# A hybrid decoder block on one core: a quarter of the expert rows streamed and multiplied densely in place of gathered

## The chip, the cores and the metric

The kernel runs on one core of one Trainium2 chip. The metric is device time in microseconds, the median of several executions. PE is the matmul engine, PEld its weight loads, DVE the vector engine, ACT the scalar engine, POOL the engine that issues gathers, SP the engine that issues most plain DMAs.

## The reference

For 256 tokens of width 2048 the layer computes, in float32:

```
h = rms_norm(x, norm1_g);  z = h @ w_in
x = x + (sigmoid(gA) * pool_mixer(z) + sigmoid(gB) * sgu_mixer(z)) @ w_out
h = rms_norm(x, norm2_g)
idx, gate = product_key_top16(h @ w_q, sub_keys)       # 8 heads x 16 experts per token
act = gelu(h . expert_u[idx])                          # 128 picks per token
x = x + sum_e gate_e * act_e * expert_v[idx_e]
out = rms_norm(x, final_g)
```

There are 128 x 128 = 16384 experts; expert number = 128 * first key + second key. A row of `expert_u` or `expert_v` is 2048 float32 numbers, 8 KB.

## The kernel before

Weights come from HBM in float32 tiles of 128 x 1024 through the class `Stream` (L54 to L109): SP loads a raw tile, ACT copies each half into a rounded part `hi` (L94), DVE or POOL subtracts it to get the rest `lo` (L96), and a product is made of three single-pass matmuls (`mm3` L243, `mm3a` L248), or of two, a wide one over both activation parts and a narrow one (`mm2` L253). Four raw buffers and five buffers of each part keep the stream ahead of PE; parts are made four halves ahead.

The stages follow one another: w_v, the pool mixer (the loop that calls `run_b` at L410, whose two partial sums `joined` L275 adds on ACT and DVE, while a layer norm runs beside it on DVE), the gate stages, w_out, and w_q (the queries). In the w_q stage `token_rows` (L731) transposes the last 48 tokens back to rows and copies each group of 16 to eight partition groups by seven DMAs from the ACT queue (L748), and `scores` (L754) hands the scores of each head to `topk_head` (L565), in two halves of 128 tokens: tokens 128 to 255 first, tokens 0 to 127 kept in the list `second`. `finish_topk` (L595) turns the picks into gather indices.

Then the sweep: all of `expert_u` streams through PE for the 208 first tokens (`run_u` L783, 128 keys of 128 experts) and the scores go to `s_scratch` in HBM (`evac` L801). The last 48 tokens do without the dense scores: their rows of `expert_u` are gathered and multiplied on DVE (L672), and their rows of `expert_v` are gathered and multiplied on PE.

After the sweep, the tail. One job per token (`v_job` L680): POOL issues a gather of 128 rows of `expert_v`, 1 MB (`fetch` L643), PE multiplies them with the coefficients in eight matmuls (L688). Beside it POOL fetches, for a token further on, its 128 scores out of `s_scratch` with a gather of 4-byte elements (`element` L837); 16 tokens make a group, whose coefficients DVE and ACT compute (`coefs` L649) and whose result is normed and written (`square` L700). First come what is left of the last 48 tokens, then tokens 128 to 207, then 0 to 127. The loop at L871 sets the order: `step` (L187) issues the PE work of the oldest fetched job and the gathers of the next, four gathers ahead, in five row buffers; `work` (L203) then takes pieces of work from the list `side` against a credit in estimated microseconds. The second top-k is put into `side` when the tail begins.

## Time and profile before

| | us |
|---|---|
| median of 3 runs | 1946.9 (1944.74 to 1947.67) |
| the profiled execution | 1951.77 |
| its span in the profile | 1950.0 |
| PE busy | 1662.7 (85%) |
| PEld busy | 1217.8 (62%) |
| DVE busy | 1033.1 (53%) |
| ACT busy | 717.4 (37%) |
| POOL busy | 595.9 (31%) |

The span is what the profiler saw between the first and the last instruction; the 1.8 us around it are part of the execution's time. A busy share is an average over stages that differ, so the rows further down are cut by stage: the mixers and queries up to some 602 us, the sweep from there to 1300 us, the tail from 1300 us to the end. The granted clock (PEclk) is 1.0 at 2.4 GHz and 0.5 at 1.2 GHz; a value between is a mean over both.

### The profile page before, as it was taken

What the parts mean: (1) busy time and instruction counts of PE and PEld (TensorE: products, weight loads), DVE (VectorE), ACT (ScalarE), POOL (GpSimd) and SP (SyncE); (2) the same over time, 40 slices, a digit from 0 to 9 for tenths busy, and PEclk for the clock granted to TensorE, in tenths of its full rate; (3) what the DMA queues carried; (4) which work ended last, traced back from release to release, by engine and by line L of the source; (5) the groups of instructions that cost most, each with busy time, mean ns of one, the idle gap of its engine ahead of it and who ended that gap; (6) DMA issues with size and microseconds to landing.
All of it is one profiled execution on the core that took longest, in us unless ns stands there. A gap on an engine that the chain in (4) does not pass through costs nothing.

```text
span 1950.0 us, 28018 instructions
## 1 busy us (share of the span) xinstructions
PE 1662.7 (85%) x10242; PEld 1217.8 (62%) x10242; DVE 1033.1 (53%) x2115; ACT 717.4 (37%) x1408; POOL 595.9 (31%) x609
## 2 busy tenths in 40 slices
PE   9999999999998999999999999985666666566665
PEld 7778888888998898888998899951110111011111
DVE  7887777777788787667676666763600000000000
ACT  7546555555434444544455445430010000000000
POOL 0220000000546111111111111136666656666662
PEclk9999999999999999999999999996576666667666
DMA  8556555555576999899999999988999999999998
GB/s 285 169 158 192 188 188 189 190 187 183 186 176 198 362 348 347 333 340 341 351 341 344 345 346 341 363 307 299 364 354 357 369 356 367 358 368 362 377 366 334
DMA packets 137994, 581.73 MB, mean 298 GB/s; under 512 B 21488, under 2 KB 37872, under 8 KB 98480
## 3 DMA queue, kind: packets, MB, share of 16 engines
q0 software_dynamic: 50704, 320.22, 42.8%
q1 hardware_dynamic: 86480, 256.97, 38.1%
q10 hardware_dynamic: 672, 2.75, 1.0%
q8 instruction: 80, 1.31, 0.3%
q14 instruction: 58, 0.48, 0.1%
HBM read 561.39 MB, written 15.73 MB: 296 GB/s over the span
## 4 chain that ended last, share of the span: by engine, by line
PE 33%; issue 30%; DMA 18%; DVE 8%; POOL 8%; ACT 1%; ACTq 0%; another core or an unknown queue 0%; SPq 0%; DVEq 0%; POOLq 0%
PE acc L792 13%; DMA rows<-in_exp_v,idxV 9%; DMA raw<-in_exp_u 8%; PE acc L793 6%; PE y L688 5%; POOL se L843 4%; POOL rows L645 4%; DVE lo L96 3%; PE acc L244 1%; PE acc L246 1%; PE acc L245 1%; PE acc L796 1%; ACT hi L94 1%; PE acc L250 1%; DVE rows L672 1%
## 5 line engine op out<-in xcount | busy, mean ns | idle before, releaser
L96 DVE TENSOR_TENSOR lo<-raw,hi 128x512 fp32r<-128x512 f32 x852 | 574.4, 704 | 288.0 <-ACT hi L94 273.8
L94 ACT CAST hi<-raw 128x512 fp32r<-128x512 f32 x904 | 535.3, 621 | 425.4 <-DMA raw<-in_exp_u 157.0
L792 PE MATMUL acc<-hhl,hi 128*128 128x416 f32 x1920 | 598.9, 372 | 3.8 <-ACT hi L94 3.8
L688 PE MATMUL y<-rows,cd 128*32 128x512 f32 x2048 | 400.1, 867 | 206.7 <-DMA rows<-in_exp_v,idxV 178.7
L793 PE MATMUL acc<-hhl,lo 128*128 128x208 f32 x1920 | 500.4, 261 | 17.8 <-DVE lo L96 17.3
L645 POOL DMA_INDIRECT rows<-in_exp_v,idxV x256 | 248.7, 972 | 513.2 <-DVE rows L672 310.7
L793 PEld LDWEIGHTS acc<-hhl,lo 128*128 128x128 f32 x1920 | 369.9, 193 | 27.5 <-DVE lo L96 26.7
L792 PEld LDWEIGHTS acc<-hhl,hi 128*128 128x128 f32 x1920 | 364.7, 190 | 35.7 <-ACT hi L94 29.1
L688 PEld LDWEIGHTS y<-rows,cd 128*32 128x32 f32 x2048 | 57.2, 130 | 502.9 <-DMA rows<-in_exp_v,idxV 376.2
L258 PE MATMUL acc<-hhl,hi 128*128 128x512 f32 x768 | 271.0, 397 | 1.9 <-ACT hi L94 1.8
L843 POOL DMA_INDIRECT se<-s_scratch,idxS x208 | 197.8, 951 | 65.5 <-issue 61.6
L260 PE MATMUL acc<-hhl,lo 128*128 128x256 f32 x720 | 202.5, 281 | 5.4 <-DVE lo L96 5.4
L654 DVE TENSOR_TENSOR cx<-se,rstd 128x16 f32<-128x16 f32 x13 | 2.3, 179 | 367.0 <-DMA se<-s_scratch,idxS 295.4
L258 PEld LDWEIGHTS acc<-hhl,hi 128*128 128x128 f32 x768 | 142.7, 188 | 32.3 <-ACT hi L94 2.9
L655 ACT ACTIVATE cx<-cx 128x16 f32<-128x16 f32 x16 | 3.5, 217 | 411.0 <-DVE cx L654 357.1
L260 PEld LDWEIGHTS acc<-hhl,lo 128*128 128x128 f32 x720 | 135.9, 189 | 10.0 <-DVE lo L96 8.4
L645 POOL DMA_INDIRECT rows<-in_exp_rows,idxU x48 | 52.4, 1092 | 228.9 <-DVE rows L672 122.5
L538 POOL DMA_DIRECT2D keys<-in_keysT x1 | 0.6, 563 | 370.1 <-PE acc L304 370.1
L672 DVE SCALAR_TENSOR_TENSOR rows<-rows,h2n 128x2048 f32<-128x2048 f32 x48 | 109.6, 2284 | 0.0
L714 DVE RECIPROCAL rt<-rt 128x1 f32<-128x1 f32 x16 | 2.6, 164 | 174.4 <-ACT rt L713 151.6
L96 POOL TENSOR_TENSOR lo<-raw,hi 128x512 fp32r<-128x512 f32 x52 | 71.9, 1394 | 64.9 <-ACT hi L94 57.0
L258 PE MATMUL acc<-mhl,hi 128*128 128x512 f32 x256 | 89.0, 395 | 0.0
(191 smaller groups left out, 1752.4 us busy)
## 6 DMA issues: line engine op xcount, KB each, us to landing
raw<-in_exp_u SPq DMA_DIRECT2D x256, 512.0 KB
raw<-in_w_in SPq DMA_DIRECT2D x96, 512.0 KB
raw<-in_w_out SPq DMA_DIRECT2D x32, 512.0 KB
raw<-in_w_q SPq DMA_DIRECT2D x32, 512.0 KB
s_scratch<-es SPq DMA_DIRECT2D x32, 416.0 KB
raw<-in_w_gproj SPq DMA_DIRECT2D x16, 512.0 KB
raw<-in_w_v SPq DMA_DIRECT2D x15, 512.0 KB
rows<-in_exp_v,idxV POOLq DMA_INDIRECT x256
```

Source lines behind the costliest of these rows:

```text
L94: self.nc.scalar.copy(h, t)
L96: eng.tensor_sub(l, t, h.bitcast(F32))
L244: nc.tensor.matmul(ps, whi, ahi, start=first, stop=False)
L245: nc.tensor.matmul(ps, whi, alo, start=False, stop=False)
L258: nc.tensor.matmul(ps, whi, both, start=first, stop=last)
L260: nc.tensor.matmul(ps[:, :T], wlo, act[:, 0], start=False, stop=False)
L645: nc.gpsimd.indirect_dma_start(out=r, out_offset=None, in_=src, in_offset=bass.IndirectOffsetOnAxis(ap=idx, axis=0))
L672: V.scalar_tensor_tensor(r, r, 1.0, h2n[g], op0=ALU.mult, op1=ALU.mult, accum_out=act[g][:, n:n + 1])
L688: nc.tensor.matmul(y[q * GQ:(q + 1) * GQ], cd[:, m * GQ:(m + 1) * GQ], r[:, q * 512:(q + 1) * 512], start=(m == 0), stop=(m == GT - 1))
L792: nc.tensor.matmul(o2, whi[:, w], hhl[:, k, :, 0:ND], start=(k == 0), stop=False)
L793: nc.tensor.matmul(o1, wlo[:, w], hhl[:, k, 0, 0:ND], start=False, stop=False)
L843: nc.gpsimd.indirect_dma_start(out=se[t0][:, m:m + 1], out_offset=None, in_=flat, in_offset=bass.IndirectOffsetOnAxis(ap=idxS[:, t0 + m:t0 ...
```

## The change

Rows of `expert_v` of the last 32 first keys (experts 12288 to 16383, 33.6 MB) are no longer gathered for the first 208 tokens. The gathers of those tokens have a bounds check that skips such rows, and a coefficient `gM` that is zero for them. In their place the 32 x 128 rows stream through a second `Stream`, and `dense_part` multiplies them for all 208 tokens at once: it builds one-hot tables on DVE (`at`, `bt`) and turns them into a dense gate table on PE (52 pieces of four tokens), reads the stored scores of these keys back from HBM (8 chunks, 3.4 MB), and makes 128 pieces of six matmuls each. The tail's loop issues 1.6 credits of these pieces at every step. Groups of tokens that end before the dense part is done are copied out of PSUM to SBUF (at most nine) and finished later, one every three steps (`release`), with an addition of the dense result by matmul (`add_dense`). Of the eight PSUM banks two stay for general use, two hold the tokens' results and four the dense sums.

Three smaller edits come along. The top-k of the first 128 tokens is put into `side` at key 30 of the sweep, with a credit of 0.17 per weight tile in place of 0.95. The pool mixer uses three matmuls per block (`whole=True`) and no `joined`. The seven copies per group in `token_rows` go to the SP queue, two `work` calls later, and the table `wide` is built before the queries and no longer in `finish_topk`.

The cut diff (left out: names of pools and a few allocations):

```diff
@@ -44,6 +44,10 @@
 KB = 4
+NF = 32
+SECOND = 30
+SLOW_CREDIT = 0.17
+PE_CREDIT = 1.6
 SHARE = (2, 3)
...
@@ -406,10 +413,10 @@
         ps = bank()
-        run_b(ps, hhl, KC, 0.3)
+        run_b(ps, hhl, KC, 0.3, whole=True)
         z = sgt.tile([P, 16 + T], F32, name="z")
         nc.gpsimd.memset(z[:, 0:16], 0.0)
-        V.tensor_mul(z[:, 16:], joined(sgt, ps), rstd)
+        V.tensor_mul(z[:, 16:], ps[:, :T], rstd)
         g = c // 2
...
@@ -538,6 +547,9 @@
     idf = tk.tile([P, TB, NH, TOPK], F32, name="idf")
+    wide = tk.tile([P, NG // GT, REP, GT], F32, name="wide")
+    for g in range(NG // GT):
+        V.tensor_copy(wide[:, g], ident[:, None, P - NG + g * GT:P - NG + (g + 1) * GT].to_broadcast([P, REP, GT]))
     io16 = tk.tile([P, TOPK], F32, name="io16")
@@ -607,17 +619,13 @@
         if tb == TB - 1:
-            wide = tk.tile([P, NG // GT, REP, GT], F32, name="wide")
-            for g in range(NG // GT):
-                V.tensor_copy(wide[:, g], ident[:, None, P - NG + g * GT:P - NG + (g + 1) * GT]
-                              .to_broadcast([P, REP, GT]))
-            yield 3.0
             pt = bank()
             yield 0.3
-            own = tk.tile([P, NG // GT, P // REP, REP], F32, name="own")
+            own = tkt.tile([P, 2 * TOPK * TOPK], F32, name="oh", bufs=1)
+            own = own[:, 0:NG * REP].rearrange("p (g n r) -> p g n r", g=NG // GT, r=REP)
             V.tensor_mul(own, pt[:, 0:(NG // GT) * P].rearrange("p (g r n) -> p g n r", g=NG // GT, r=REP),
@@ -630,6 +638,8 @@
         V.tensor_copy(idxV[:, ts], pt[:, 0:P])
+        V.scalar_tensor_tensor(gM[:, tb * P:tb * P + nd], pt[:, 0:nd], float((NK - NF) * P), gT[:, tb * P:tb * P + nd],
+                               op0=ALU.is_lt, op1=ALU.mult)
         V.scalar_tensor_tensor(idxS[:, tb * P:tb * P + nd], pt[:, 0:nd], float(ND), tpos[:, tb * P:tb * P + nd],
@@ -640,10 +650,10 @@
-    def fetch(src, idx):
+    def fetch(src, idx, **kw):
         r = rp.tile([P, D], F32, name="rows")
         nc.gpsimd.indirect_dma_start(out=r, out_offset=None, in_=src,
-                                     in_offset=bass.IndirectOffsetOnAxis(ap=idx, axis=0))
+                                     in_offset=bass.IndirectOffsetOnAxis(ap=idx, axis=0), **kw)
         return r
@@ -653,7 +663,7 @@
         S.activation(x, x, AF.Gelu_apprx_tanh)
-        V.tensor_mul(cd[:, 0::GQ + 1], x, gT[:, t0:t0 + GT])
+        V.tensor_mul(cd[:, 0::GQ + 1], x, (gM if t0 < ND else gT)[:, t0:t0 + GT])
         yb[t0] = [cd, None]
@@ -686,16 +696,48 @@
                 nc.tensor.matmul(y[q * GQ:(q + 1) * GQ], cd[:, m * GQ:(m + 1) * GQ], r[:, q * 512:(q + 1) * 512],
-                                 start=(m == 0), stop=(m == GT - 1))
+                                 start=(m == 0), stop=(m == GT - 1 and not (t0 < ND and "done" in dense)))
             if m == 0:
             if m == GT - 1:
-                later(lambda: square(y, t0))
-
-        return lambda: fetch(exp_v, idxV[:, t:t + 1]), consume
+                if t0 >= ND:
+                    later(lambda: square(y, t0))
+                else:
+                    grouped(y, t0)
+        if t >= ND:
+            return lambda: fetch(exp_v, idxV[:, t:t + 1]), consume
+        return lambda: fetch(exp_v, idxV[:, t:t + 1], bounds_check=(NK - NF) * P - 1, oob_is_err=False), consume
+    dense = {}
+    waiting = []
+    def add_dense(y, t0):
+        tb, o = divmod(t0, P)
+        for q in range(NQ):
+            nc.tensor.matmul(y[q * GQ:(q + 1) * GQ], dense["pick"][:, o:o + GQ],
+                             dense["out"][tb][:, q * 512:(q + 1) * 512], start=False, stop=True)
+    def grouped(y, t0):
+        if "done" in dense:
+            add_dense(y, t0)
+            later(lambda: square(y, t0))
+        else:
+            ys = dense["pool"].tile([P, 512], F32, name="ys", bufs=dense["kept"])
+            waiting.append((t0, ys))
+            assert len(waiting) <= dense["kept"]
+            later(lambda: S.copy(ys, y))
+    def release():
+        t0, ys = waiting.pop(0)
+        y = bank()
+        nc.tensor.matmul(y, ident, ys, start=True, stop=False)
+        add_dense(y, t0)
+        later(lambda: square(y, t0))
@@ -744,8 +786,12 @@
                     yield 2
-                for r in range(1, REP):
-                    S.dma_start(h2n[g][r * GT:(r + 1) * GT], h2n[g][0:GT])
+                def copies(g=g):
+                    for r in range(1, REP):
+                        nc.sync.dma_start(h2n[g][r * GT:(r + 1) * GT], h2n[g][0:GT])
+                later(copies, 2)
@@ -794,8 +840,9 @@
                     nc.tensor.matmul(o2, whi[:, w], hhl[:, k, :, 0:ND], start=False, stop=True)
-            work(TK_CREDIT)
-
+            work(rate[0])
+    rate = [TK_CREDIT]
     keep = {}
@@ -819,6 +866,10 @@
             clock[2] = LAST_PACE
+        if i == SECOND:
+            rate[0] = SLOW_CREDIT
+            side.extend(second)
+            side.append(finish_topk(0))
         ps = bank()
@@ -829,6 +880,101 @@
+    tk_stack.close()
+    hh_stack.close()
+    hn_stack.close()
+    psA_stack.close()
+    psA[0] = pool(ps_stack, "psB", 2, space=PSUM)
+    psD = pool(ps_stack, "psD", 4, space=PSUM)
+    dp = pool(ctx, "dp")
+    dense["pool"] = dp
+    dense["kept"] = 9
+    dense["out"] = [dp.tile([P, D], F32, name=f"yd{tb}") for tb in range(TB)]
+    V.memset(dense["out"][TB - 1], 0.0)
+    dense["pick"] = dp.tile([P, P + GQ - GT], F32, name="pick")
+    V.memset(dense["pick"], 0.0)
+    V.tensor_copy(dense["pick"][:, 0:P], ident)
+    vst = Stream(nc, rawp, hip, lop)
+    for half in range(2):
+        for j in range(NF):
+            e = (NK - NF + j) * P
+            vst.add(exp_v[e:e + P, half * GP:(half + 1) * GP])
+    gates = dp.tile([P, NF, ND], F32, name="gates")
+    DT = 4
+    NC = 4
+    def dense_part():
+        ab = dp.tile([P, 2, ND], U32, name="ab")
+        abf = dp.tile([P, 2, ND], F32, name="abf")
+        V.tensor_scalar(ab[:, 0], idxV[:, 0:ND], 7, None, op0=ALU.logical_shift_right)
+        V.tensor_scalar(ab[:, 1], idxV[:, 0:ND], NK - 1, None, op0=ALU.bitwise_and)
+        V.tensor_copy(abf, ab)
+        ps = None
+        for t in range(0, ND, DT):
+            at = dp.tile([P, DT, NF], F32, name="at", bufs=2)
+            bt = dp.tile([P, DT, NK], F32, name="bt", bufs=2)
+            V.tensor_tensor(at, abf[:, 0, t:t + DT, None].to_broadcast([P, DT, NF]),
+                            iota[:, None, NK - NF:NK].to_broadcast([P, DT, NF]), op=ALU.is_equal)
+            for m in range(DT):
+                V.tensor_scalar(bt[:, m], iota, abf[:, 1, t + m:t + m + 1], gT[:, t + m:t + m + 1],
+                                op0=ALU.is_equal, op1=ALU.mult)
+            yield 0.3 * DT
+            if t % GT == 0:
+                ps = bank()
+            for m in range(DT):
+                nc.tensor.matmul(ps[:, (t % GT + m) * NF:(t % GT + m + 1) * NF], bt[:, m], at[:, m],
+                                 start=True, stop=True)
+            if (t + DT) % GT == 0:
+                later(lambda ps=ps, t0=t - t % GT: S.copy(
+                    gates[:, :, t0:t0 + GT], ps[:, 0:GT * NF].rearrange("p (t j) -> p j t", j=NF)))
+        yield 1.0
+        def chunk(j):
+            ks = slice(j, j + NC)
+            x = dp.tile([P, NC, ND], F32, name="sx", bufs=2)
+            nc.sync.dma_start(x, s_dram[(NK - NF + j) * P:(NK - NF + j + NC) * P].rearrange("(k j) t -> j k t", j=P))
+            yield
+            V.tensor_mul(x, x, rstd2[:, None, 0:ND].to_broadcast([P, NC, ND]))
+            S.activation(x, x, AF.Gelu_apprx_tanh)
+            yield
+            V.tensor_mul(gates[:, ks], x, gates[:, ks])
+            yield
+        def parts(j):
+            hi = dp.tile([P, ND], F32R, name="chi", bufs=3)
+            lo = dp.tile([P, ND], F32R, name="clo", bufs=3)
+            S.copy(hi, gates[:, j])
+            V.tensor_sub(lo, gates[:, j], hi.bitcast(F32))
+            return hi, lo
+        for j in range(0, NF, NC):
+            for _ in chunk(j):
+                yield 0.5
+        for half in range(2):
+            acc = [[psD.tile([P, 512], F32, name="dacc") for f in range(2)] for tb in range(TB)]
+            ready = parts(0)
+            for j in range(NF):
+                chi, clo = ready
+                for f in range(2):
+                    whi, wlo = vst.next()
+                    if f == 0 and j < NF - 1:
+                        ready = parts(j + 1)
+                    for tb in range(TB):
+                        ts = slice(tb * P, min(ND, (tb + 1) * P))
+                        mm3a(acc[tb][f][0:ts.stop - ts.start], chi[:, ts], clo[:, ts], whi, wlo,
+                             j == 0, j == NF - 1)
+                    yield 1.36
+            for tb in range(TB):
+                n = min(ND, (tb + 1) * P) - tb * P
+                for f in range(2):
+                    d = half * GP + f * HG
+                    S.copy(dense["out"][tb][0:n, d:d + HG], acc[tb][f][0:n])
+        yield 1.0
+        dense["done"] = True
     flat = s_dram.rearrange("e (t o) -> (e t) o", o=1)
@@ -836,8 +982,6 @@
         t0, m = elems.pop(0)
-        while side and t0 < P:
-            work(V_CREDIT)
         if m == 0:
@@ -866,13 +1010,28 @@
         jobs.append(with_elements(v_job(t), 1))
-    side.extend(second)
-    side.append(finish_topk(0))
+    part = dense_part()
+    owed = 0.0
+    since = 0
     while fetched or jobs:
         work(V_CREDIT)
+        owed += PE_CREDIT
+        while "done" not in dense and owed > 0:
+            try:
+                owed -= next(part)
+            except StopIteration:
+                break
+        since += 1
+        if "done" in dense and waiting and since >= 3:
+            release()
+            since = 0
+    for _ in part:
+        pass
+    while waiting:
+        release()
+        drain()
     drain()
-    tk_stack.close()
     ps_stack.close()
```

## Rows read from the trace of the kernel before

**Rows 1.** the page: DMA share in tenths, 40 slices of 48.75 us
```profile
DMA  8556555555576999899999999988999999999998
```

**Rows 2.** windows: length; busy PE, PEld, DVE, ACT, POOL; PEclk; DMA share; GB/s
```profile
602.00:1300.00 698.00, 673.54 (x4452) 622.67 (x4455) 485.73 (x786) 335.64 (x648) 108.87 (x96) 0.99 0.90 338
1300.00:1342.00 42.00, 22.81 (x127) 3.30 (x115) 19.34 (x87) 1.67 (x3) 27.76 (x29) 0.59 0.83 292
1342.00:1932.00 590.00, 370.77 (x2064) 73.47 (x2061) 66.76 (x263) 48.94 (x79) 374.40 (x396) 0.65 0.95 364
1932.00:1950.00 18.00, 8.40 (x42) 1.06 (x34) 0.91 (x2) 0.95 (x3) 0.43 (x1) 0.69 0.47 190
```

**Rows 3.** timeline of POOL inside the tail: start, length, instruction, idle before
```profile
1375.80 0.94 POOL L645 DMA_INDIRECT rows<-in_exp_v,idxV  x1 [2.81 <-PE y L688]
1377.04 0.94 POOL L843 DMA_INDIRECT se<-s_scratch,idxS  x1 [0.30 <-issue]
1378.28 0.95 POOL L645 DMA_INDIRECT rows<-in_exp_v,idxV  x1 [0.30 <-issue]
```

**Rows 4.** groups of instructions from 1342 to 1932 us
```profile
L688 PE MATMUL y<-rows,cd 128*32 128x512 f32 x1620 | 333.4, 909 | 184.3 <-DMA rows<-in_exp_v,idxV 158.4 <-issue 25.7
L645 POOL DMA_INDIRECT rows<-in_exp_v,idxV x206 | 194.3, 943 | 160.6 <-PE y L688 75.5 <-remote 41.7 <-issue 41.2
L843 POOL DMA_INDIRECT se<-s_scratch,idxS x190 | 180.5, 950 | 57.9 <-issue 56.4 <-DMA rows<-in_exp_v,idxV 1.5
```

**Rows 5.** window in which the last tokens, without element gathers, are fetched
```profile
1895.00:1920.00 25.00, 17.10 (x114) 3.90 (x106) 1.29 (x6) 2.45 (x5) 11.68 (x13) 0.64 1.01 416
```

**Rows 6.** groups on POOL inside the sweep
```profile
L645 POOL DMA_INDIRECT rows<-in_exp_v,idxV x39 | 44.0, 1128 | 345.8 <-DVE rows L672 310.7 <-PE y L688 35.0
```

**Rows 7.** timeline of PE across the end of the sweep
```profile
1299.40 4.50 PE L688 MATMUL y<-rows,cd 128*32 128x512 f32 x40
...
1310.85 1.94 PE L688 MATMUL y<-rows,cd 128*32 128x512 f32 x8 [2.25 <-DMA rows<-in_exp_v,idxV]
```

**Rows 8.** timeline of PE in the first stage, streamed weight as moving operand
```profile
21.73 0.39 PE L249 MATMUL acc<-hi,hhl 128*128 128x512 f32 x1
...
22.41 0.39 PE L249 MATMUL acc<-hi,hhl 128*128 128x512 f32 x1
```

**Rows 9.** timeline of PE, four score matmuls with 128 by 128 stationary parts
```profile
514.58 0.60 PE L757 MATMUL acc<-keys,qt 128*128 128x128 f32 x4
```

**Rows 10.** timeline of PE in the pool mixer, two pairs of matmuls
```profile
56.02 0.40 PE L258 MATMUL acc<-hhl,hi 128*128 128x512 f32 x1
...
56.37 0.40 PE L258 MATMUL acc<-hhl,hi 128*128 128x512 f32 x1
```

**Rows 11.** timeline of PE in the query stage, two threes of matmuls
```profile
512.06 0.28 PE L244 MATMUL acc<-hhl,hi 128*128 128x256 f32 x1
...
512.42 0.28 PE L244 MATMUL acc<-hhl,hi 128*128 128x256 f32 x1
```

**Rows 12.** waits of PE in the pool mixer: us in total, times, longest
```profile
PE acc L260 <- DVE lo L96: 5.4, 9, 1.5
```

**Rows 13.** timeline of ACT, one group of the h2n copies
```profile
559.56 9.86 ACTq L748 DMA_DIRECT2D h2n<-h2n  x7
```

**Rows 14.** waits of PE from 545 to 625 us
```profile
PE acc L617 <- DVE wide L612: 2.8, 3, 1.4
PE acc L246 <- DVE lo L96: 2.4, 1, 2.4
```

**Rows 15.** windows with much DVE work: two of the sweep, one of the tail
```profile
700.00:725.00 25.00, 24.69 (x162) 23.78 (x160) 22.28 (x33) 13.09 (x26) 3.44 (x3) 1.00 0.96 362
750.00:775.00 25.00, 25.00 (x169) 24.87 (x168) 21.86 (x33) 13.01 (x25) 3.44 (x3) 1.00 0.98 361
...
1300.00:1425.00 125.00, 74.85 (x406) 14.81 (x394) 67.13 (x284) 10.79 (x17) 82.13 (x86) 0.62 0.88 329
```

**Rows 16.** waits of PE in the whole sweep
```profile
PE acc L793 <- DVE lo L96: 17.3, 24, 1.4
```

More of the change, by code (lines that the diff above doesn't have):

```diff
@@ L506, in block_kernel @@
     gT = gs.tile([P, T], F32, name="gT")
+    gM = gs.tile([P, ND], F32, name="gM")
     tpos = gs.tile([P, ND], F32, name="tpos")
@@ L527, in block_kernel @@
     rp = pool(ctx, "rp", ROWS, side="right")
-    hn = pool(ctx, "hn", side="right")
     yp = pool(ctx, "yp", 2, side="right")
-    evp = pool(ctx, "evp", 2, side="right")
+    hn_stack = ExitStack()
+    hn = pool(hn_stack, "hn", side="right")
+    evp = pool(hn_stack, "evp", 2, side="right")
     act = [hn.tile([P, P // REP], F32, name=f"act{g}") for g in range(NG // GT)]
```

9 lines of the change are left out of this document (6 added, 3 removed).

## The prediction

> **What bounds the kernel now.** I read the page's slices first: the DMA share is nine tenths or more from the start of the sweep almost to the end, and half of that before [rows 1]. Then the windows by stage [rows 2]. The sweep takes 698 us with PE busy for 673.5 of them: PE-bound, DMA close behind at 0.90. The tail takes 650 us: 42 us for what is left of the last 48 tokens, 590 us in which the gathers of 208 tokens are issued, 18 us from the last gather to the end. In the 590 us the DMA share is 0.95 at 364 GB/s and PE is granted 0.65 of its clock, so DMA bounds it: 590 / 208 = 2.84 us per token of 1.049 MB (128 rows of 8 KB), or 1.049 / 364 GB/s = 2.88. But a second limit lies close below. POOL issues gather and element gather in turn, 0.94 us each and 0.30 us between, a gather every 2.48 us, until the five row buffers are full, and then waits 2.8 us for PE to free one [rows 3]; in sum its gathers waited 160.6 us, its element gathers only 57.9 [rows 4]. A change that takes bytes out gains only down to about 2.5 us per token. Where the last 16 tokens have no element gathers, DMA reaches 416 GB/s [rows 5].
>
> **The tail, step by step.** Counted with the reference on its own inputs, 25.1% of the first 208 tokens' picks fall on the last 32 keys. A gather keeps 96 of 128 rows, 0.786 MB; 208 gathers lose 54.7 MB, and 33.6 MB of streamed rows and 3.4 MB of scores come in. Net 17.7 MB, 49 us at 364 GB/s. That much can't be had, as these bytes are not spread evenly. The pieces' own credits tell where they fall, at 1.6 per step: tables 52 x 1.2 + 1 = 63.4 (39.6 steps), score chunks 12 (7.5 steps), dense pieces 128 x 1.36 = 174 (109 steps). The first 14 steps serve the last 48 tokens, whose gathers skip nothing: 42 us as before.
> - Tables, 26 more steps. DMA would need 0.786 / 364 = 2.16 us, POOL 2.5. DVE now works beside it, and gathers issued in the sweep beside a busy DVE took 1.13 us, not 0.94 [rows 6], so I take 2.6: 68 us (2.5 to 2.7: 65 to 70). What the SBUF page of the Trainium skill says (Who interferes with whom) is that a DVE instruction in a two-port mode shuts POOL out for its whole length; no row shows which of the new ones are such.
> - Score chunks, 7.5 steps: (0.786 + 0.454 MB) / 364 = 3.4 us each, 26 us.
> - Dense, 109 steps: 0.786 + 33.6 / 109 = 1.094 MB, 3.00 us each: 327 us. At the 416 GB/s of [rows 5] it would be 2.63 (287 us); the other end is the first rival's 3.36 (366 us).
> - The other 66 steps: 50 at POOL's 2.5 = 125 us, 16 without elements at 0.786 / 416 = 1.9 us or PE's 1.94 [rows 7]: 31 us.
>
> Together 577 us against 590: -13. What follows the last gather stays as it is, but for one `add_dense` (matmuls like a token's, 0.9 us): +1.
>
> What must hide. PE: a token costs 0.90 us at 2.4 GHz (five in 4.50) and 1.94 us at 1.2 GHz [rows 7]. A dense matmul follows the next after 0.227 us (three in 0.68) [rows 8]: 1.36 per piece, 1.18 pieces per step, so 1.60 + 0.90 = 2.50 us of the 3.00. A table matmul is two instructions like those of [rows 9], at most 0.15 each; 5.25 tokens per step, 1.6 + 0.9 = 2.5 of 2.6, tight. A release is two passes of a token's size (1.8 us at full clock, 3.9 at half) every three steps: 4.5 or 9.7 us against 7.5. With the clock granted in between I add 0.5 us to each of nine: +4 (0 to 20). ACT and DVE: 1.18 pairs of casts and subtractions per step, under 1.7 us together, beside engines that the tail leaves idle. Without that cover they would stand in front of PE. On DVE `coefs` waits for its elements, and the `lo` parts of the stream stand behind it in the queue. The elements are issued right after a gather four tokens ahead, and PE has four parts in hand, 3.4 steps. So both wait for the same landing; I take 0 (at worst half a step, 1.5 us, in each of seven groups: 10). On SP the score chunks and weight tiles stand behind no output: no group is finished before the dense part is done, except the last tokens' three.
>
> **Before the sweep.** Pool mixer: a block goes from 0.35 us as a pair [rows 10] to 0.36 as a three [rows 11]; 128 blocks, +1.3. Eight `joined` additions leave DVE, for which PE waited 5.4 us there [rows 12]; I take 3 of them back: -2 (-4 to +1). The copies: one group of seven holds ACT for 9.9 us [rows 13], and PE then waited 2.4 us for a part that came late [rows 14]. On SP they stand ahead of raw tiles instead, and four raw buffers are 32 blocks, 11.5 us of PE, so most of it stays covered: -2 (-4 to +4). `wide` left PE waiting 2.8 us [rows 14] and now stands before the first query: -2 (-3 to +2). Sum -6.
>
> **The sweep.** The second top-k brings its DVE time along: 67.1 us in the tail's first 125 us [rows 15], less some 5 us of coefficients and outputs. Its credit, 55 at 0.68 per key, spreads it over 81 keys of 5.45 us: 3.5 us more in each 25, on top of 485.7 / 698 x 25 = 17.4 [rows 2]. Two windows that already had 22 us of DVE work show PE at 24.7 and 25.0 [rows 15], so the PE has stood this much. PE waited 17.3 us for `lo` in the whole sweep [rows 16]; I add a sixth: +3 (0 to +15). In the tail its removal gives nothing, since nothing waited for DVE there.
>
> **Sum.** -6 + 3 - 13 + 1 + 4 = -11. The profiled execution took 1951.8 us, 4.9 above the median, so 1940.8 becomes **1936** on the median's scale.
>
> **Rivals.**
> 1. *The skipped rows leave the 16 DMA engines unequal: slower.* A gather is done when its fullest engine is. If each engine keeps its own eight rows, it has 6.0 left on average, but the fullest of five gathers in a row (the buffers) has 6.8 to 7.4, depending on which rows go together, by the same count of picks. With 7.07, near the middle, a token needs 2.84 x 7.07 / 8 = 2.51 us and the streamed 0.308 MB another 0.85: 3.36 per dense step, +39 us: 1975. It decides from 3.10 us per step on, where the 11 us are gone. For it: the before kernel has no slack between share 0.95 and full. Against it: two queues fill each other's holes. The DMA page of the Trainium skill (The descriptor swizzle) has engines bound to destination partitions in such eights, which speaks for this rival; in the trace only whole gathers are to be seen.
> 2. *The stream fills DMA better than gathers do.* At 416 GB/s the dense steps take 287 us: 1936 - 40 = 1896. For it: [rows 5]; against it: there no element gathers ran.
> 3. *A skipped row is not free* (it is moved, or its place in the queue costs as much). Then 26 x 2.84 + 7.5 x 4.1 + 109 x (1.049 + 0.308) / 364 + 50 x 2.84 + 16 x 2.52 = 693 us, +116 on the forecast: 2052. No row shows a bounds check; nothing speaks for it but that.
> 4. *PE stays at 1.2 GHz and becomes the bound.* A dense step then takes 1.94 + 1.60 x 1.94 / 0.90 = 5.4 us: 109 x 2.4 = +260, 2196. Against it: in the sweep, with PE this busy, the granted clock was 0.99 [rows 2].
>
> **Chances.** Forecast 0.47, rival 1 0.28, rival 2 0.16, rival 3 0.05, rival 4 0.04. A measurement of this kernel tells some 0.2% (4 us) from no change. Of the forecast's 0.47, 0.34 lie below -4 us, 0.08 within, 0.05 above; of rival 1, which may come in part, 0.03 below, 0.05 within, 0.20 above; rival 2 is faster, 3 and 4 slower. So faster 0.53, same 0.13, slower 0.34. The likeliest case alone: 1915 to 1955 (the sweep's and releases' upper bounds; half the way to rival 2). The range has to reach near rivals 1 and 2: 1893 to 1975.
>
> **What would show it.** In the changed profile: 2.5 to 2.6 us between gathers while the tables are built and after the dense part, DMA share well under 0.95 there; some 3.0 in the dense part, with PE near full clock; a sweep of about 700 us; no 9.9 us of ACT in the copies. Over 3.1 us per dense step with DMA share clearly under 0.95 and PE waiting for rows speaks for rival 1. It is wrong if tail gathers move 1 MB still (GB/s and bytes of the software queue), if PE is busy throughout at a low clock, or if the sweep has grown by more than 15 us.

## The result, and the profile after

The change made the kernel slower: 2008.66 us (2005.19 to 2022.93, 4 runs) against 1945.82 us (1941.16 to 1947.67, 4 runs) of the kernel before, a ratio of 1.0341 (95% interval 1.0287 to 1.0394). Forecast were 1936 us and a range up to 1975. The profiled execution took 2010.08 us, 58 more than that of before. A ratio given without an interval rests on a single run.

The page of the kernel after, busy tenths of PE, PEclk, DMA and GB/s in 40 slices of 50.2 us, and the software queue's row (packets, MB, share of 16 engines):

```profile
PE   9999999999998999999999999999759999997765
...
PEclk9999999999998999999999999765879999998877
DMA  8556566665588998999999999666889999998787
GB/s 287 166 174 188 187 191 187 190 188 191 159 209 301 365 372 324 370 356 354 349 353 369 359 334 364 235 207 216 277 301 359 336 363 326 327 341 273 237 273 277
...
q0 software_dynamic: 50704, 265.45, 36.6%
```

Where [rows 1] had nine tenths to the end, the DMA share falls to six tenths in three slices behind the sweep, and PE fills up there at a low clock. The skipped rows are really not moved: the queue's bytes were 320.22 MB before. The tail by stage, after (columns as in [rows 2]): tables, score chunks, dense part, releases, the rest.

```profile
1283.00:1434.00 151.00, 142.62 (x784) 86.90 (x785) 71.68 (x270) 12.74 (x21) 83.56 (x86) 0.61 0.66 221
1434.00:1477.00 43.00, 14.39 (x108) 4.65 (x108) 15.73 (x18) 9.58 (x15) 23.90 (x19) 0.62 0.88 294
1477.00:1817.00 340.00, 324.25 (x1828) 145.84 (x1831) 111.52 (x214) 99.13 (x208) 216.24 (x215) 0.98 0.93 337
1818.00:1898.00 80.00, 55.03 (x368) 16.24 (x370) 9.07 (x30) 14.03 (x34) 46.56 (x48) 0.83 0.75 253
1898.00:2008.00 110.00, 70.74 (x424) 14.60 (x424) 5.41 (x17) 9.36 (x18) 55.91 (x57) 0.73 0.77 274
```

Cut at the last key of the sweep, the last table matmul and the first and last dense one, the two traces and the forecast compare so (us):

| stretch | before | forecast | after | after less forecast |
|---|---|---|---|---|
| up to the end of the sweep | 1299.8 | 1297 | 1278.4 | -18 |
| rest of the last 48 tokens, tables | | 42 + 68 = 110 | 156 | +46 |
| score chunks | | 26 | 42 | +16 |
| dense part | | 327 | 340 | +13 |
| all behind it | | 156 + 18 + 1 + 4 = 179 | 192 | +13 |
| the whole tail | 650 | 642 | 730 | +88 |

88 - 18 is 70, and -11 + 70 the 58 us by which the profiled executions differ (to rounding). So the early part gained more than forecast, and every stretch of the tail missed, the tables most.

**Tables.** Groups of the kernel after from 1300 to 1414 us:

```profile
L928 PE MATMUL acc<-at,bt 128*128 128x32 f32 x306 | 61.5, 363 | 5.9 <-DVE bt L922 4.7 <-issue 1.2
...
L698 PE MATMUL y<-rows,cd 128*32 128x512 f32 x224 | 47.2, 931 | 0.0
L922 DVE TENSOR_SCALAR bt<-iota,abf,gT 128x128 f32<-128x128 f16 x148 | 41.4, 364 | 0.0
L987 POOL DMA_INDIRECT se<-s_scratch,idxS x34 | 32.3, 950 | 10.4 <-issue 10.4
L655 POOL DMA_INDIRECT rows<-in_exp_v,idxV x28 | 28.2, 1006 | 43.9 <-PE y L698 38.2 <-PE acc L928 3.9 <-issue 1.8
```

PE is busy almost throughout (61.5 + 47.2 of 114 us, and the windows above have 142.6 of 151), but at a granted clock of 0.61, most of it at 1.2 GHz. POOL waits 38.2 us for PE to free a row buffer, so the gathers come late.

**Chunks.** The longest wait of PE between 1420 and 1480 us (in total, times, longest), and DVE's timeline in the same stretch:

```profile
PE dacc L256 <- ACT hi L98: 21.9, 1, 21.9
```

```profile
1430.54 1.01 DVE L940 TENSOR_TENSOR sx<-sx,rstd 128x832 f32<-128x832 f32 x1
1431.61 0.48 DVE L663 MEMSET cd<- 128x512 f32 x1
1442.57 0.17 DVE L664 TENSOR_TENSOR cx<-se,rstd 128x16 f32<-128x16 f32 x1 [10.47 <-issue]
...
1443.18 1.02 DVE L943 TENSOR_TENSOR gates<-sx,gates 128x832 f32<-128x832 f32 x1
...
1457.05 1.03 DVE L940 TENSOR_TENSOR sx<-sx,rstd 128x832 f32<-128x832 f32 x1 [4.52 <-DMA sx<-s_scratch]
```

DVE stands 10.5 us before `cx`, the first instruction of `coefs` that reads the gathered scores (the profile puts this wait down to "issue", the same wait of 10.3 us in a_again and e9 to the scores' DMA). The product of the first chunk, whose gelu was done on ACT at 1436.1, stands behind it in the queue until 1443.2. After that the chunks come one by one, since two buffers allow no more: DVE waited 11.3 us in all for their loads. ACT's parts `hi` of the streamed rows stand behind the chunks' gelu, and PE behind `hi`.

**Releases.** The same again, in the timelines of DVE and PE after the dense part (`rt` is the norm of a finished group):

```profile
1858.29 0.17 DVE L664 TENSOR_TENSOR cx<-se,rstd 128x16 f32<-128x16 f32 x1 [16.29 <-DMA se<-s_scratch,idxS]
...
1860.34 2.08 PE L738 MATMUL acc<-ys,ident 128*128 128x512 f32 x2 [7.72 <-ACT rt L755]
```

### The profile page after: what moved, and what is told of

Its sections match the earlier page's. It is cut to its first block, busy times and chain, and to the rows that moved or that the text cites. A ratio compares the mean times of both kernels' runs of the same rounds, so it can differ in the third digit from the quotient of the medians.

```text
span 2008.4 us, 32122 instructions
## 1 busy us (share of the span) xinstructions
PE 1861.6 (93%) x11676; PEld 1411.6 (70%) x11676; DVE 1209.9 (60%) x2585; ACT 817.0 (41%) x1614; POOL 615.8 (31%) x607
## 4 chain that ended last, share of the span: by engine, by line
PE 50%; issue 27%; DMA 11%; POOL 5%; DVE 5%; ACT 1%; another core or an unknown queue 0%; SPq 0%; POOLq 0%; DVEq 0%; ACTq 0%
PE acc L838 15%; PE y L698 8%; PE acc L839 7%; DMA raw<-in_exp_u 5%; DMA rows<-in_exp_v,idxV 4%; PE acc L928 4%; POOL rows L655 3%; POOL se L987 2%; PE dacc L256 2%; PE acc L251 2%; PE acc L253 2%; PE acc L252 2%; DVE lo L100 2%; PE dacc L258 2%; PE dacc L257 2%
## 5 line engine op out<-in xcount | busy, mean ns | idle before, releaser
L100 DVE TENSOR_TENSOR lo<-raw,hi 128x512 fp32r<-128x512 f32 x982 | 662.0, 701 | 381.7 <-ACT hi L98 323.1
L98 ACT CAST hi<-raw 128x512 fp32r<-128x512 f32 x1032 | 616.0, 619 | 551.7 <-PE acc L838 130.8
L838 PEld LDWEIGHTS acc<-hhl,hi 128*128 128x128 f32 x1920 | 362.3, 189 | 37.3 <-ACT ev L863 23.5
L698 PE MATMUL y<-rows,cd 128*32 128x512 f32 x2048 | 320.3, 696 | 43.2 <-DMA rows<-in_exp_v,idxV 34.4
L265 PE MATMUL acc<-hhl,hi 128*128 128x512 f32 x640 | 226.2, 396 | 1.6 <-ACT hi L98 1.6
L267 PE MATMUL acc<-hhl,lo 128*128 128x256 f32 x600 | 168.7, 281 | 1.3 <-DVE lo L100 1.3
L256 PE MATMUL dacc<-hi,chi 128*128 128x512 f32 (+1 forms) x256 | 114.7, 448 | 34.7 <-ACT hi L98 26.2
L265 PEld LDWEIGHTS acc<-hhl,hi 128*128 128x128 f32 x640 | 119.0, 188 | 26.5 <-ACT hi L98 2.0
L256 PEld LDWEIGHTS dacc<-hi,chi 128*128 128x128 f32 (+1 forms) x256 | 43.8, 171 | 131.1 <-issue 57.7
L928 PEld LDWEIGHTS acc<-at,bt 128*128 128x128 f32 x416 | 77.2, 280 | 63.0 <-DVE bt L922 31.4
L251 PE MATMUL acc<-hhl,hi 128*128 128x256 f32 x384 | 111.4, 290 | 0.0
L253 PE MATMUL acc<-hhl,lo 128*128 128x256 f32 x384 | 109.5, 285 | 1.4 <-DVE lo L100 1.4
```

The costliest lines, as they stand in the source:

```text
L98: self.nc.scalar.copy(h, t)
L100: eng.tensor_sub(l, t, h.bitcast(F32))
L251: nc.tensor.matmul(ps, whi, ahi, start=first, stop=False)
L256: nc.tensor.matmul(ps, ahi, whi, start=first, stop=False)
L265: nc.tensor.matmul(ps, whi, both, start=first, stop=last)
L267: nc.tensor.matmul(ps[:, :T], wlo, act[:, 0], start=False, stop=False)
```

## The experiments

Runs were spread over several chips, and the kernel before differs among them: medians of 1946 us beside the result and 1943 beside e1, e2, e4 and b6, but 1888, 1892, 1888 and 1890 beside the others. So ratios are to the kernel before on the same chip. What differs is the gathers: where [rows 2] moved 364 GB/s, the kernel with the early edits alone (b5) moved 404 on a faster chip, 2.6 us per token.

```profile
1300.00:1830.00 530.00, 339.73 (x2056) 60.09 (x2060) 70.38 (x284) 49.07 (x80) 378.30 (x400) 0.69 1.01 404
```

There DMA is full at 1.01, and POOL's 2.5 us lie only 0.1 us below. One more thing sets the slower chip apart: POOL's gathers stand there for something that the profile calls "remote" and can't name (41.7 us in the tail of before, 36.8 in that of b6, 7 to 11 in the changed kernels), and never on the faster chips. What it is stays open.

### The table stage

Theory A: the table steps are bound by PE at a low granted clock. Theory B: the order of SP's queue and the chunks make the loss.

**e1_no_tables**

```diff
-            V.tensor_tensor(at, ...)
-                V.tensor_scalar(bt[:, m], ...)
+            V.memset(gates[:, j:j + 4], 0.0)
             yield 0.3 * DT
-                nc.tensor.matmul(ps[...], bt[:, m], at[:, m], start=True, stop=True)
```

> Leaves out the 416 table matmuls and the one-hot tables on DVE (the dense gates are zero, so the streamed keys add nothing to the output); the pieces keep their credits, so everything else stands at the same step. Theory A (the table matmuls and the tokens' matmuls, both at 1.2 GHz, fill PE and set the table steps at 4.1 us): the stretch from the sweep's end to the last table credit falls from 156 us to about 110, the whole to 1965 (1960 to 1972). Rival (POOL beside a busy DVE, or DMA, sets these steps): it stays above 140 us, the whole above 1995.

1987.32 against 1943.11 us (ratio 1.023), between the two expectations. The stretch from the end of the sweep to the dense part, chunks included, took 165 us (after: 198), the whole tail 699 (730), though PE still stood 19.4 us in front of the dense part. Window:

```profile
1287.00:1432.00 145.00, 82.08 (x482) 15.45 (x479) 20.64 (x35) 9.85 (x15) 97.83 (x97) 0.68 0.83 281
```

PE is no longer the bound there, though the clock is no more than 0.68. Without the tables' work the tail is 31 us shorter, about half of the 46 + 16.

**e2_weights_first**

```diff
         yield 1.0
+        for _ in range(RAW_BUFS):
+            vst.load()
```

> Loads the first four raw tiles of the streamed rows before the score chunks, so that they no longer stand behind the eight chunk loads on SP; all else as in the changed kernel. Theory B (the 22 us in which PE waits for the first dense weight are SP's order: chunk loads wait for their two buffers, and the weights wait behind them): PE's wait falls below 6 us, the whole to 1991 (1986 to 1995). Rival (DMA has these bytes to move anyway and the time comes back in the dense steps): within 5 us of 2009.

2026.17 us (1.043); PE stood 20.1 us in front of the dense part. SP's order is not the cause. The whole time says nothing of the edit: the table stage, which comes before the edited line, took 169 us in this run, at a clock of 0.52.

**e4_filler**: work added, to see the clock alone.

```diff
+            for _ in range(3):
+                nc.tensor.matmul(fl, wzf[:, 0:P], wzf, start=True, stop=True)
             for m in range(DT):
                 nc.tensor.matmul(ps[...], bt[:, m], at[:, m], start=True, stop=True)
```

> Adds work: three wide half-precision matmuls of zeros (512 columns, nothing reads them) before each of the 52 table pieces, 0.64 us per piece at 2.4 GHz, 1.3 us at 1.2 GHz. Theory A in its clock form (the table steps are slow because the clock stays at 1.2 GHz though PE is busy): the clock rises to 2.4 GHz there, the table steps fall from 4.1 to 3.0 to 3.3 us, the whole to 1975 (1968 to 1985). Rival (the clock stays, PE only has more to do): the table steps rise to about 6 us, the whole to 2075 (2060 to 2090).

1994.70 us (1.027). Window of the table stage:

```profile
1282.00:1421.00 139.00, 130.15 (x938) 75.96 (x938) 71.38 (x267) 12.74 (x21) 83.46 (x86) 0.93 0.73 240
```

With 156 more matmuls the granted clock is 0.93 and no longer 0.61, as A has it; the filler costs most of what the clock gives. The stage is 12 us shorter than in the kernel after, but unedited it took from 133 to 169 us in single runs, so the gain in time isn't shown; on another chip there was none (e8 below). What settles A is the product of busy time and clock, in windows that hold the table stage:

| run | window | PE busy | clock | product |
|---|---|---|---|---|
| after | 151 | 142.6 | 0.61 | 87.0 |
| a_again | 133 | 124.8 | 0.70 | 87.3 |
| e2_weights_first | 169 | 164.0 | 0.52 | 85.3 |
| e5_chunks_spread | 152 | 149.7 | 0.57 | 85.3 |
| e9_four_sx | 151 | 148.8 | 0.57 | 84.8 |
| e10_coefs_late | 118 | 117.0 | 0.76 | 88.9 |

The work is 85 to 89 us at full clock, and the stage is as long as the granted clock makes it.

### The smaller edits

**b6_early_second**: the kernel before with the three early edits and the earlier top-k, no stream. **b5_early**: the three early edits alone. **b7_second**: the earlier top-k alone. All are parts of the diff as it stands.

> The kernel before with the smaller edits alone: three matmuls per block in the pool mixer, the copies from the SP queue, the early table, and the second top-k inside the sweep; no streamed rows, the tail gathers all rows. Theory C (the 21 us that the changed kernel is ahead at the end of the sweep come from these edits alone): 1924 (1918 to 1930). Rival (they come from the memory layout that the dense part forced, or from chance): 1938 to 1948.

> The kernel before with three edits alone: three matmuls per block in the pool mixer, the copies from the SP queue, the early table; the second top-k stays in the tail. Theory C1 (these three bring nearly all that the kernel with both brought, and the top-k in the sweep costs nothing and brings nothing): 1923 (1918 to 1928), sweep about 680 us. Rival C2 (half of it comes from taking the top-k out of the tail): 1930 to 1938, sweep 690 us or more.

> The kernel before with the second top-k inside the sweep alone (early edits left out). Theory C1: 1943 (1939 to 1948), as the kernel before. Rival C2: 1930 to 1936.

b6: 1922.39 us, ratio 0.991 (0.988 to 0.9941). b5: 1865.23, 0.9885 (0.984 to 0.993). b7: 1890.14, 1.0006 (0.9981 to 1.0031). The gain is the three edits'; moving the top-k costs nothing and brings nothing. b5 and b6 beat both kernels, by some 1% the kernel before.

**b8_pool, b9_copies, b10_wide**: the three edits one by one.

> The kernel before with the pool mixer's three matmuls per block alone. Prediction's step: -2 (-4 to +1). If each edit brings only what its own wait was worth, the last z of the mixer comes at some 107.5 in place of 110.6 us, the sweep keeps its 698 to 703 us, and the time is 3 us under the kernel before (ratio 0.998). If the shorter sweep comes from here, the sweep is under 690 us and the ratio under 0.993.

> The kernel before with the seven copies per group of 16 tokens issued from SP, two pieces of work later, alone. Prediction's step: -2 (-4 to +4). Theory of the copies: ACT no longer stands 9.9 us per group, the query stage ends 5 to 9 us earlier, the rows of the last 48 tokens start earlier, so that the DVE work beside the sweep is done earlier and PE waits less for lo: sweep 680 us in place of 700, ratio 0.988 to 0.992. Rival: the query stage alone gains 2 to 5 us and the sweep keeps 698 to 703 us: ratio 0.997 to 0.999.

> The kernel before with the table built ahead of the queries (and its product in a shared buffer) alone. Prediction's step: -2 (-3 to +2). If only its own wait of 2.8 us goes: ratio 0.998 to 1.000, sweep 698 to 703 us. If the sweep's gain comes from here (3.0 of credit less in the list, so all later pieces run earlier): sweep under 690 us, ratio under 0.993.

| run | us | ratio | sweep's first matmul begins, last ends, between them |
|---|---|---|---|
| before (another chip) | | | 595.6, 1299.5, 704 |
| b8_pool | 1881.78 | 0.9966 (0.9945 to 0.9987) | 593.9, 1294.6, 701 |
| b9_copies | 1878.93 | 0.9962 (0.9943 to 0.9981) | 588.4, 1288.2, 700 |
| b10_wide | 1877.80 | 0.9950 (0.9933 to 0.9967) | 595.7, 1283.1, 687 |

The three ratios multiply to 0.988, b5's own. The pool mixer's last `z` came 2.5 us earlier, near the 2 of the forecast; the copies brought the sweep forward by 7 us; and `wide` made the sweep itself shorter. Waits of PE from the start of the sweep on, first b8_pool, then b10_wide:

```profile
PE acc L793 <- DVE lo L96: 17.0, 25, 1.3
```

```profile
PE acc L792 <- DVE lo L96: 5.9, 12, 1.2
```

11 us of waits for `lo` go with it. Why is argued only: the U products (2.28 us on DVE) fall at another place among the parts of the stream once the list of pieces is 3.0 of credit shorter. No run tried another shift.

### The wait ahead of the dense part

**e5_chunks_spread**

```diff
             for _ in chunk(j):
-                yield 0.5
+                yield 1.2
```

> The changed kernel with 1.2 in place of 0.5 credits per piece of a score chunk: the eight chunks spread over 18 steps in place of 7.5, everything else in its order. Loading the weights earlier did not shorten PE's 22 us before the first dense matmul. Theory B2 (the eight chunks are a chain of load, scale, gelu and multiply through two buffers, about 4 us each on DVE, ACT and DMA, longer than the 7.5 steps that cover it, and the first weight's cast stands behind it on ACT): the gap falls below 5 us, the whole to 1990 (1984 to 1996). Rival (the first weight tiles come late whatever the order): the gap stays above 15 us, the whole within 6 of 2009.

1982.27 against 1887.84 us (1.050). The wait was 9.8 us, but the dense part began 65 us behind the last table, not 42: the wait was filled with steps, and the chain was no shorter. Both theories missed the wait.

**e9_four_sx**

```diff
-            x = dp.tile([P, NC, ND], F32, name="sx", bufs=2)
+            x = dp.tile([P, NC, ND], F32, name="sx", bufs=4)
```

> The changed kernel with four buffers for the score chunks in place of two. Chain of the buffers: from the second chunk on each load waits for the product of the chunk two before it, five us a chunk; with four buffers the loads overlap, the eight chunks need some 20 us less, the wait of PE before the first dense matmul falls from 20 to under 10 us, and the stretch from the last table matmul to the first dense one from 42 to some 30; ratio to the kernel before some 1.028 in place of 1.034. Rival (the queues of the gathers and of DVE and ACT set it, not the buffers): the wait stays at 18 to 24 us and the ratio at 1.034.

Wait 12.7 us, the stretch 35 us: a good third of the wait, as the chain of the buffers has it, but not all. The ratio, 1.0451 (1.0419 to 1.0484), says nothing of it: in the profiled run the tables drew a clock of 0.57 and took 152 us, where a_again's took 133. DVE in this run:

```profile
1433.97 0.48 DVE L663 MEMSET cd<- 128x512 f32 x1
1444.75 0.17 DVE L664 TENSOR_TENSOR cx<-se,rstd 128x16 f32<-128x16 f32 x1 [10.29 <-DMA se<-s_scratch,idxS]
```

The 10 us at the head of DVE's queue were still there. That made the last theory: `coefs` is issued in the step that issues the last gather of its scores, and so it waits for that gather wherever POOL is late.

**e10_coefs_late**, and **e11_late_four** with e9's edit as well:

```diff
         if m == GT - 1:
-            coefs(se[t0], t0)
+            later(lambda: coefs(se[t0], t0), 4)
```

> The changed kernel with the coefficients of a group of 16 tokens issued four steps after the last of its scores' gathers, in place of right behind it. Theory of the head of the queue: VectorE no longer waits 10 us on the scores in the chunk stage, nor 16 in the releases; PE's wait before the first dense matmul falls from 20 to 22 us to 10 to 13, its waits for rt in the releases from 10 to under 4 us; the tail is 10 to 18 us shorter (ratio some 0.007 lower than the changed kernel's 1.034 to 1.045). Rival (the two buffers alone make the wait): it stays at 18 to 22 us, the ratio at 1.034 to 1.045.

> The changed kernel with both edits: coefficients four steps later and four buffers for the chunks. If the wait before the dense part is made by these two alone, it falls to 0 to 5 us, the stretch from the last table matmul to the first dense one from 42 to under 26 us (the 7.5 steps at 2.6 to 3.4 us that were forecast), and the ratio is some 0.012 lower than the changed kernel's. If a third cause is there (weights, SP), it stays over 8 us. The tables stay as they are: some 130 to 150 us, by the granted clock, so the kernel stays slower than the one before.

e10: 1926.03 us, ratio 1.0209 (1.0165 to 1.0252). e11: 1915.46, 1.0147 (1.012 to 1.0174). By stretch, from the profiled runs (us; all but the first two columns are from faster chips, for which the forecast was not made):

| stretch | forecast | after | a_again | e9 | e10 | e11 |
|---|---|---|---|---|---|---|
| end of sweep to last table | 110 | 156 | 138 | 157 | 123 | 125 |
| chunks | 26 | 42 | 44 | 35 | 42 | 26 |
| dense part | 327 | 340 | 330 | 333 | 316 | 319 |
| behind it | 179 | 192 | 171 | 173 | 168 | 166 |
| tail | 642 | 730 | 683 | 697 | 650 | 635 |

The wait ahead of the dense part fell to 13.3 us with the later `coefs` and to 2.8 with both, and the chunks then take the 26 us of the forecast. But the one edit reaches further. DVE's wait at the same `cx` in e11:

```profile
1414.58 0.17 DVE L664 TENSOR_TENSOR cx<-se,rstd 128x16 f32<-128x16 f32 x1 [1.91 <-DMA se<-s_scratch,idxS]
```

In the dense part the steps fall to 316 / 109 = 2.90 us: on ACT, too, the parts `chi` of the gates stand behind the gelu of `coefs`, and PE's waits for them go, first a_again, then e10:

```profile
PE dacc L256 <- ACT chi L949: 9.4, 4, 4.7
```

```profile
PE dacc L256 <- ACT chi L949: 0.2, 1, 0.2
```

In the kernel after, e5 and e9 they are 7.6 to 11.8 us, in e11 0.7. In the releases PE's waits for `rt` fall from 10.2 to 3.5 us. In the table stage PE's waits for `bt` are 3.9 us (6.1 to 12.1 in the kernel after, a_again and e9), and the granted clock is 0.76, where the runs without the edit had 0.52 to 0.70; but the clock differs from run to run, and no unedited run of the changed kernel was made on that chip. So of the 33 us by which e10's tail is shorter than a_again's, twice what I had expected, the 15 in the table stage aren't shown to be the edit's.

### The dense part

**a_again** (the changed kernel once more, beside the next two) and **e7_two_matmuls**:

```diff
-                        mm3a(acc[tb][f][0:ts.stop - ts.start], chi[:, ts], clo[:, ts], whi, wlo,
-                             j == 0, j == NF - 1)
+                        o = acc[tb][f][0:ts.stop - ts.start]
+                        nc.tensor.matmul(o, chi[:, ts], whi, start=j == 0, stop=False)
+                        nc.tensor.matmul(o, chi[:, ts], wlo, start=False, stop=j == NF - 1)
```

> The changed kernel once more, beside the next three on one chip: their reference. The chip of the last four runs was faster at gathers (the kernel before 1888 us, 2.59 us per step of the tail). If this one is like the first: 2009 (2003 to 2016); if like the second: 1985 (1975 to 1995), for there the tail of the kernel before sits on POOL and the changed one gains nothing from fewer bytes.

> The dense pieces make two of their three matmuls (the rest part of the gates times the rounded weights is left out; the output is less exact); all loads, casts and subtractions stay. Theory E (the dense steps of 3.1 us are bound by PE: 1.18 pieces of 1.40 us and a token of 1.18 us between full-width matmuls, 2.83, and transposes): the dense stretch falls from 340 to 290 to 320 us, the whole by 20 to 50. Rival 1 of the prediction (DMA with unequal engines binds there): it stays above 333 us, the whole within 8.

1959.69 and 1965.03 us against 1892.35 (1.036, 1.038). The windows of their dense parts, a_again first:

```profile
1457.00:1787.00 330.00, 319.28 (x1828) 144.49 (x1832) 112.71 (x215) 100.71 (x210) 212.06 (x216) 0.98 0.95 351
```

```profile
1470.00:1793.00 323.00, 271.25 (x1572) 104.39 (x1575) 110.46 (x214) 99.53 (x210) 222.47 (x216) 0.93 0.96 358
```

256 matmuls less, 48 us of PE less, and only 7 us won, between the two expectations. PE's waits in that window of e7 show where the rest went (a_again has 9.4 us of the first and 0.7 of the second):

```profile
PE dacc L968 <- ACT chi L949: 30.4, 8, 6.4
...
PE y L698 <- DMA rows<-in_exp_v,idxV: 20.6, 26, 1.9
```

So two next limits stand a few us behind PE: the queue behind `coefs`, and DMA at a share of 0.96. In the kernel as it stands PE is the bound all the same. In a_again the gathers wait 91.7 us for PE in the dense part, PE 0.7 us for rows, and in e10, without the waits for `chi`, PE is busy in 314.8 of 316 us:

```profile
1438.00:1754.00 316.00, 314.79 (x1826) 143.95 (x1825) 113.03 (x214) 101.72 (x210) 212.41 (x215) 0.99 0.96 364
```

**e6_skip_only** and **e6_again** (b6 with the skipping gathers, nothing streamed):

```diff
+        return lambda: fetch(exp_v, idxV[:, t:t + 1], bounds_check=(NK - NF) * P - 1, oob_is_err=False), consume
```

> The kernel before with all the smaller edits, and with the skipping gathers but nothing streamed: the last 32 keys' share of the first 208 tokens is left out of the output. Theory D (skipped rows are free for DMA, and POOL's two issues, 1.01 + 0.95 + 0.60 us, bound the step): 2.56 us per step, DMA share near 0.8, the whole 1870 (1862 to 1880). Rival 1 of the prediction (the fullest engine binds): at least 2.7 us per step, above 1890. Rival 3 (a skipped row costs as much as a moved one): 2.85 us, 1915 to 1925.

> The skipping gathers without the stream again (the last 32 keys' share of the first 208 tokens is left out), since on the second chip the kernel before already ran at 2.59 us per step, so that 2.56 us there told little of DMA. On a chip where the kernel before needs 2.84: theory D 2.56 us per step and 1870 (1862 to 1880); rival 1 at least 2.7; rival 3 2.85 and 1915 or more. On a chip like the second one: 1855 to 1862 again.

1858.92 us against 1887.84 (0.985) and 1857.21 against 1892.35 (0.981), single runs on two of the faster chips. Without the skips b5 took 1865 (1862.91 to 1869.16) on the first of them. So on such a chip the skipping is worth only some 6 us, hardly more than the spread of b5's runs, even when nothing is paid for it: a step takes 2.56 us and no less. The groups of e6_skip_only from 1300 to 1830 us:

```profile
L650 POOL DMA_INDIRECT rows<-in_exp_v,idxV x208 | 209.0, 1005 | 69.7 <-issue 40.9 <-PE y L693 26.3 <-PE acc L715 1.2
L857 POOL DMA_INDIRECT se<-s_scratch,idxS x202 | 191.0, 946 | 61.6 <-issue 56.7 <-DMA rows<-in_exp_v,idxV 4.6 <-DMA se<-s_scratch,idxS 0.3
```

POOL is busy for 400 of the 530 us, and of the 131 idle ones 97.6 (40.9 + 56.7) are its own pause of 0.3 us behind each instruction: it is the floor, as the forecast had it from [rows 3].

On the first, slower chip, for which the forecast was made, no run has the skips without the stream; e1 comes near it. With no table work beside them, its 27 gathers from 1343 to 1416 us came 2.76 us apart on average, less than the 2.84 of before. They come in runs at POOL's pace,

```profile
1391.69 1.01 POOL L655 DMA_INDIRECT rows<-in_exp_v,idxV  x1 [0.30 <-PE y L698]
...
1394.25 1.00 POOL L655 DMA_INDIRECT rows<-in_exp_v,idxV  x1 [0.30 <-issue]
...
1396.81 1.00 POOL L655 DMA_INDIRECT rows<-in_exp_v,idxV  x1 [0.30 <-PE y L698]
```

with pauses of up to 2.7 us between the runs, in which POOL waits for PE to free a buffer. So a part of rivals 1 and 3 isn't excluded there.

**e8_all_mended** (e4's filler, e5's spread, a release every five steps):

> The changed kernel with the fillers in the table steps, the chunks spread over 18 steps and the releases every five steps. Theories A and B2 add up: 14 us from the clock, 15 to 20 from the gap, 5 to 10 from the releases, so 35 to 45 us below the changed kernel on the same chip, still above the kernel before, as the dense steps cost 3.1 us. Rival (the gains overlap, PE has the same work to do): less than 25 us below.

1967.97 us (1.040), 8 us above a_again and not 35 to 45 below: 137 us of tables at a clock of 0.90, where a_again needed 133 at 0.70.

## Why the prediction was wrong

Two steps failed by their mechanism: the cover of the table steps, which was priced at a clock that was not granted, and the wait of `coefs` at the head of DVE's queue, which was put at nothing. The dense steps came near their number for another reason than the one given.

**"On DVE `coefs` waits for its elements ... So both wait for the same landing; I take 0 (at worst half a step, 1.5 us, in each of seven groups: 10)."** This step failed. I had named the queue, and then let both sides wait for the same gather. But POOL falls behind the issue order where PE is late, and the one instruction at the head of DVE's queue then stood 10.5 us in the chunks and 16.3 in the releases. Behind it stood not four `lo` parts that PE had in hand, but what PE waited for next: `bt`, the chunk products, `rt`, and on ACT `chi`. One edit to it took the tail from 683 to 650 us, between chips of like speed, 15 us of it in the table stage, where its part isn't shown. A view of before that the prediction left unused has such waits already, those of DVE from 1300 to 1930 us:

```profile
DVE cx L654 <- DMA se<-s_scratch,idxS: 295.4, 10, 33.3
```

Up to 33 us each, harmless there: most of each is DVE with nothing else to do while 16 tokens are gathered, so they show the place and not the price. The change filled that queue.

**"Tables, 26 more steps ... I take 2.6: 68 us", with "5.25 tokens per step, 1.6 + 0.9 = 2.5 of 2.6, tight".** The stage of this step missed by most, 46 of the 88 us. The cover was priced at 2.4 GHz. The work was no more than forecast (87 us at full clock in a stretch forecast at 110), the clock was lower: granted were 0.52 to 0.76, and PE became the bound. The tail of before had shown 0.59 to 0.65 [rows 2]. Rival 4 was this mechanism, but I placed it in the dense steps, where the clock was indeed 0.98, and argued it away by the sweep [rows 2]. Even with `coefs` mended the stage is 13 to 15 us over the forecast. What the SBUF page of the Trainium skill (Who interferes with whom) says of DVE shutting POOL out, weighed there, isn't to be seen: the gathers took 1006 ns beside the busy DVE, 1005 in e6 without it.

**"Score chunks, 7.5 steps ... 26 us."** Priced by bytes. Eight chunks through two buffers are a chain of latencies; with the head of the queue and the buffers mended it is 26 us.

**"Dense, 109 steps ... 3.00 us each: 327."** 3.12 in the kernel after (DMA share 0.93), 3.03 in a_again, 2.90 in e10: the number nearly held, but by luck, since it was priced by bytes and PE binds. "1.60 + 0.90 = 2.50 us of the 3.00" is the term that was too small: PE was busy for 324.25 / 109 = 2.97 us a step. In the timeline of the kernel after a one-piece step took 2.58 us and a two-piece one 3.98 (1604.87 to 1607.45, 1600.89 to 1604.87), so a piece costs 1.40 and a token 1.18 us, not the 0.90 of [rows 7], which hold five tokens in a row. Rival 1 (3.36) and rival 2 (2.63) did not come at their size; with PE in front, a smaller part of either can't be told.

**"The other 66 steps", and "+4" for the releases.** 13 us over. PE waited 10.0 + 3.9 + 2.7 us there for `rt` and `sq`; in a_again these waits are 14.6 us, in e10 8.2. And the 45 gathers up to the last element gather came 3.2 us apart on average, not 2.5: POOL stood 19.0 us for PE to free a buffer and 7.2 us for the "remote" releaser. In a_again they came 2.8 us apart.

**Before the sweep "-6", the sweep "+3".** -7 and -14. The queries' last score matmul came 7 us earlier (594.1 for 600.8, in b9 593.6), by the copies, which I had put at -2; `wide` was put at -2 by its own wait of 2.8 us, and its place in the list of pieces was not counted.

**Rival 3** (a skipped row is not free) was right in a part. From b5 to e6 the packets under 512 B rise by 6689, and 6689 rows of 8 KB are the 54.8 MB that went: a skipped row still counts as a small packet. The pages of both, b5 first:

```profile
DMA packets 137995, 581.75 MB, mean 313 GB/s; under 512 B 21488, under 2 KB 37872, under 8 KB 98480
...
q0 software_dynamic: 50704, 320.22, 44.0%
```

```profile
DMA packets 137996, 526.99 MB, mean 284 GB/s; under 512 B 28177, under 2 KB 44561, under 8 KB 105169
...
q0 software_dynamic: 50704, 265.45, 40.5%
```

The queue's engine time fell by 0.440 x 1861.2 x 16 - 0.405 x 1857.2 x 16 = 1068 us, or 0.16 us per skipped row. Rows make up most of the 13103 us before; if all of it were the 38912 rows, a moved one took 0.34. So by this estimate up to half of a row's time stays. It is not the full price: a dense step would then have taken (1.049 + 0.308) / 364 = 3.73 us, and it took 3.12.

What stays open: the kernel after lost 63 us on its chip, a_again 67 on a faster one, where the tail of before is shorter too. Whether e11 with the faster tail beats the kernel before on a chip where gathers move 364 GB/s wasn't tried; against b5 or b6 it would have to win another 1%. What lowers the clock in the table stage, and by how much in which run, is open too.

## What to carry to other kernels

Before work is added to an idle engine, list the long waits at the head of its queue, harmless ones too: the new work can stand behind them, and an issue order that lets a consumer follow its gather directly is safe only while nothing else shares the queue. Price cover on PE at the clock that the trace grants in that stage, not at that of another stage with the same busy share. And look for the second bound before valuing saved bytes: with POOL's floor at 2.5 us per token and gathers at 2.6, as on the faster chips, a quarter of the rows skipped for nothing is worth some 6 us.

## What the runs showed of the hardware

A gather that skips rows took POOL 1.005 us to issue in place of 0.94 [rows 3], and a skipped row still cost up to half of a moved one's DMA time, by the estimate above. The granted clock stayed at 1.2 GHz for most of a stage in which PE was 94% busy, with two instructions for every 128 by 32 table matmul and eight narrow ones per token, and it differed between runs of the same kernel on two chips (0.61, 0.70); when three matmuls of 512 columns were put in for every four of them, it was 0.93. The chips differ by 10% in how fast the same gathers go (366 GB/s in b6, 404 in b5, from 1300 to 1830 us), and only on the slower one POOL stood for a "remote" releaser.
